# A fp32 transformer stack on one core: three modulation units, two pairs' transposes and products, and a table load are given other places in the attention

## The chip, the cores and the metric

One core of one Trainium2 chip runs the whole program. The time is the device time of one execution in microseconds (us), here the median of three runs. TensorE (PE) does matrix products, VectorE (DVE) and ScalarE (ACT) the elementwise work, GpSimd (POOL) almost nothing, and the queue of SyncE (SP) issues nearly all loads.

## The reference

Two blocks run one after the other on 256 tokens of width 1024, all in fp32. The first has two layers, the second one. Each layer of the first block normalizes, shifts and scales its input with columns of `mod`, mixes tokens (layer 0 by pooling, layer 1 by attention), adds the result through a gate, and does the same around an MLP. The second block is a mix of a gated delta net with a forgetting attention, followed by another MLP. The change lies in layer 1's attention, and by its text in the second block's gates.

```python
mod = c_act @ w_mod[i] + b_mod[i]            # c_act = silu(c), 1 x 1024
sh1, sc1, g1, sh2, sc2, g2 = split(mod, 6)
h = modulate(rmsnorm(x, norm_mix[i]), sh1, sc1)
q, k, v = split(h @ w_qkv, 3)                # 16 heads of 64
logit = q @ k.T / 8 + t5_bias                # causal: one block holds the 256 tokens
o = softmax(logit) @ v
x = x + g1 * (o @ w_o)
h = modulate(rmsnorm(x, norm_mlp[i]), sh2, sc2)
x = x + g2 * (relu(h @ w_up) ** 2 @ w_down)
```

With 256 tokens and blocks of 256, no block lies in the past, so the reference's choice of blocks leaves plain causal attention.

## The kernel before, in words

**Products.** A fp32 product runs as three products of a faster fp32 format: each operand is split into a high part and the rest. For a weight, a piece of 128 x 1024 is loaded as `_r`, ACT copies it into the high part `_h` (line 245), and DVE subtracts to get the low part `_l` (line 251). PE needs both. Pieces that are split within the buffers of the modulation columns carry `_m` or `_p` instead, and have to wait until such a buffer is free.

**Modulation columns.** A unit (`wmc112` to `wmc117` in the attention) is one load of a megabyte, two passes of DVE over it (`column`, line 440) that multiply it with `c_act` and sum along it, and one small fix-up (line 444). None of these columns is needed in the attention; they are for the layer's MLP. Such units are taken one at a time from a list, `pending`, by `ride` (line 944). In the attention the function `riding` (line 1174) calls it, and `riding` itself is called at the end of each of the eight projections of queries and keys and of the two quarters of values, ten calls in all, with six units to hand out: it calls `ride(4)` each time, and the first six calls find one.

**The attention** (`attention`, line 1144). Sixteen heads are worked as eight pairs. PE's program there is: products with `h` for the values and for `qk` (queries and keys, from `wqk`, four projections a half), between them the pairs' scores `s`, transposes `pt` of the softmax's rows, and products `pv` with the values, and last the output products `wo`. `pt5` is head 5's transposes, and `pv2` belongs to heads 4 and 5. Where the small pieces stand among the wide products is set by a clock that counts the estimated cost of the wide steps (`beside`), and a table `events` of (time, piece): a pair's scores are due at `H_S + H_P * head`, its transposes `H_T` after them (`H_TL` for the last four heads), its `pv` `H_V` after the second head's transposes. `until_head` issues all pieces up to a head without regard to the clock. In the attention PE runs in exactly this order (`InOrder`, line 281).

```python
at = H_S + H_P * hd if hd < 12 else max(H_S + H_P * hd, 36.0 + H_S + H_L * (hd - 12))
lag, by = (H_T, H_P) if hd < 12 else (H_TL, H_L)
events += [(at, hd, scores, pr), (at + lag, hd, transposes, hd), (at + lag + by, hd + 1, transposes, hd + 1),
           (at + lag + by + H_V, hd + 1, pv, pr)]
```

**A head's way.** PE writes the scores; DVE adds the bias and takes each row's maximum (`softmax_rows`, line 1110), negates it (line 1112); ACT takes exp with a sum (line 1113); DVE takes reciprocals (line 1114) and scales (line 1115); PE transposes (`pt`); ACT copies the transposed rows to `pT` (line 1210); PE multiplies with the values (`pv`); ACT and DVE split the result into `att_o_hi` and `att_o_lo` (lines 977, 978), which the `wo` products read. Each head has two row blocks, so that sm00 and sm01 are those of head 0, and sm120 the first of head 12.

**The order of the other engines** is set by a scheduler when the program is built; each engine then works its own queue strictly in that order. SP's loads too run in order: a load whose buffer is not free yet holds up those behind it.

**The second block** interleaves the computation of its gates with projections (`interleave`, line 111): after each step of the gates, `R_GATE` steps of the projection. One step of the gates gives the running sums `fc` (line 1444).

Of the kernel before, what the change touches and what calls it, by code (L numbers as in the profile page):

```python
# [8 lines left out]
F32 = mybir.dt.float32  # L9
F32R = mybir.dt.float32r  # L10
I32 = mybir.dt.int32
AF = mybir.ActivationFunctionType
ALU = mybir.AluOpType

P = 128
# [18 lines left out]
B_FIRST = 4 * 128  # L34
B_PREV = 2 * B_FIRST
B_N = B_PREV + 4 * PADW
R_GATE = 2.0
H_S = 1.0
H_P = 2.8
H_L = 2.0  # L40
H_T = 6.5
H_V = 2.0
H_TL = 5.0
DELAY = 3
C_FEAT = 0.6
T2K = 8
R_LEFT = 10
# [60 lines left out]
V_BG, V_POOL = 15, 16  # L108


def interleave(main, filler, ratio=None):

    owed = 0.0
    for r in main:
        owed += r if ratio is None else ratio
        while owed >= 1.0:
            owed -= 1.0
            next(filler, None)
    for _ in filler:
        pass  # L120
# [37 lines left out]
def build(tc, a, out):  # L158
    nc = tc.nc
    vec, act, pe, pool, sp = nc.vector, nc.scalar, nc.tensor, nc.gpsimd, nc.sync  # L160
    from contextlib import ExitStack
    ctx = ExitStack()
    with ctx:
# [4 lines left out]
        work = ctx.enter_context(tc.tile_pool(name="work", bufs=2))  # L168
# [33 lines left out]
        def later():  # L202
            st = ExitStack()
            for f in fences:
                st.enter_context(tc.issue_after(f))
            return st
# [68 lines left out]
        ones = const.tile([P, P], F32, name="ones")  # L275
# [404 lines left out]
        steps = {}  # L680
# [195 lines left out]
        for sec, hf in HALVES:  # L876
            n = f"s{sec}{hf}"
# [66 lines left out]
        def ride(left):  # L944

            if len(pending) > left:
                with later(), tc.issue_after(ride_after[0]) if ride_after else ExitStack():
                    pending.pop(0)()
# [184 lines left out]
        def attention(i, h, w0, wn):  # L1133
# [5 lines left out]
            ohl = hl_tiles("att_o", S)  # L1139
            toep_ap = toep[:, :]  # L1140
            st = {}

            def values(w, t):

                ps = mm_tile(f"v0{t}")
                token_major(w, h, t * P, P, ps)
                act.activation(vt[:, t, :512], ps, AF.Copy)

            def quarter_values(w, q):

                ps = mm_tile(f"v1{q}")
                for t in range(2):
                    for kt in range(KT):
                        mm3(ps[:, t * 256:(t + 1) * 256], hl(h, kt, slice(t * P, (t + 1) * P)),
                            w(q * 2048 + kt * 256, 256), kt == 0, kt == KT - 1)
                        if kt % 2:
                            yield 0.64
                c0 = 512 + q * 256
                act.activation(vt[:, :, c0:c0 + 256], ps.rearrange("p (t d) -> p t d", t=2), AF.Copy)
                riding()  # L1160
# [11 lines left out]
                riding()  # L1172

            def riding():
                ride(4)
                if len(sums_due) > delay[0]:
                    sums_due.pop(0)()

# [51 lines left out]
            def wo(j, t):  # L1230
                if t == 0:
                    wos.append(split_chunk(a["w_o"][j], f"wo{j}", spare=3 * j))
                ts = slice(t * P, (t + 1) * P)
                if j == 0:
                    for n in range(2):
                        wops[t, n] = (mm_tile, acc_tile)[t](f"wo{t}{n}")
                for m in range(8):
                    k, n = (m // 2, m % 2) if j else (m % 4, m // 4)
                    mm3(wops[t, n], hl(ohl, 4 * j + k, ts), wos[j](k * D + n * 512, 512), j == 0 and k == 0,
                        j == 1 and k == 3)  # L1240
                    if m % 2:
                        yield 1.28
# [3 lines left out]
            for pr in range(NH // 2):  # L1246
                hd = 2 * pr
                at = H_S + H_P * hd if hd < 12 else max(H_S + H_P * hd, 36.0 + H_S + H_L * (hd - 12))
                lag, by = (H_T, H_P) if hd < 12 else (H_TL, H_L)
                events += [(at, hd, scores, pr), (at + lag, hd, transposes, hd), (at + lag + by, hd + 1, transposes, hd + 1),  # L1250
                           (at + lag + by + H_V, hd + 1, pv, pr)]
            events.sort(key=lambda e: e[0])

            def beside(steps):

                for cost in steps:
                    clock[0] += cost
                    while events and events[0][0] <= clock[0]:
                        _, _, f, n = events.pop(0)
                        f(n)  # L1260

            def until_head(hd):
                while any(e[1] <= hd for e in events):
                    _, _, f, n = events.pop(0)
                    f(n)
# [6 lines left out]
            pe = InOrder(nc.tensor)  # L1272
            delay[0] = DELAY
            for t in range(2):
                values(w0, t)
            todo = all_projects(0)
            for steps in todo[:2]:
                for _ in steps:
                    pass
            for steps in todo[2:]:  # L1280
                beside(steps)
            todo = all_projects(1)
# [4 lines left out]
            wn.piece(0)  # L1287
            wn.piece(1)
            steps = wo(1, 0)
            for k in range(4):  # L1290
                until_head(9 + 2 * k)
                next(steps)
            next(steps, None)
            while sums_due:
                sums_due.pop(0)()
            pe = nc.tensor
# [23 lines left out]
        h = boundary(ac, lambda: gates[0, 1], *mods(1, 0), hl_tiles("att1", S), 0, "att1")  # L1320
        wu1 = Chunk(a["w_up0"], "wu10", inmraw=2)
        ac, rest = attention(1, h, wv0, wu1)
        while len(pending) > 4:
            ride(4)
# [128 lines left out]
        def conv_proj(chunk, dst, ci):  # L1453
            w = split_chunk(a["w_in"][ci], f"wi{chunk}")
            for h in range(4):
                ps = mm_tile(f"cp{chunk}{h}")[:, :T2]
                yield from costing(ws_steps(w, u, h, ps, 0, T2, 2), 0.68)
                cw = convw[:, ci * 4 + h]
                cb = row272(f"cb{chunk}{h}", T2 + 4)
                y = dst[:, h]  # L1460
                vec.memset(cb[:, 0:3], 0.0)
                act.activation(cb[:, 3:3 + T2], ps, AF.Copy)
                act.activation(y, ps, AF.Copy, scale=cw[:, 3:4])
                for j in range(3):
                    vec.scalar_tensor_tensor(y, cb[:, j:j + T2], cw[:, j:j + 1], y, ALU.mult, ALU.add)
            act.activation(dst, dst, AF.Silu)
            yield 0.0
# [390 lines left out]
        def urgent(gen):  # L1858

            while True:  # L1860
                with tc.high_priority():
                    try:
                        r = next(gen)
                    except StopIteration:
                        return
                yield r

        def early_gates():
            yield from gate_chain()
            for i in range(3):  # L1870
                yield
                gdn_decays(i)

        interleave(urgent(early_gates()), conv_proj(1, gk, 1), R_GATE)

        def rounds(fill, *gens):
# [218 lines left out]
```

## Time and profile before

| | |
|---|---|
| median of 3 runs (946.74, 948.55, 949.04) | 948.55 us |
| the profiled execution | 948.82 us |
| its span, first to last instruction | 947.0 us |
| mean granted clock of PE over the span | 0.990 of full speed |
| PE busy | 913.9 us, 97% of the span |
| DVE busy | 638.7 us, 67% |
| ACT busy | 498.2 us, 53% |
| POOL busy | 12.5 us, 1% |
| moved from and to memory | 198.31 MB, 209 GB/s in the mean |

Of an execution's 948.82 us, 947.0 lie between the first and the last instruction. All times below with a place in the program count from the first instruction. A busy share is that of the whole span. A wait is idle time of an engine, put down to the instruction that ended it. The attention's heads lie between about 275 and 375 us.

### The profile page before, as it was taken

The page shows a single profiled execution, that of the slowest core. Times are in us where ns is not written, and L with a number is a line of the kernel's source. Part 1 is how long each engine was busy: PE and PEld are TensorE (multiplying, and loading weights), DVE is VectorE, ACT ScalarE, POOL GpSimd, SP SyncE. Part 2 cuts the span into 40 slices and gives each one's busy share as a digit, 9 for nine tenths or more (in the row PEclk, how much of TensorE's full clock was granted, in tenths as well). Part 3 has the DMA queues.
Part 4 walks back from the last instruction along what each step waited for, and adds up shares of the span by engine and source line. Part 5 has one row for each costly group of instructions (what it writes and reads, how often), then busy time and mean ns, then how long its engine had stood idle before and what let it go on. Part 6 is the DMA issues. An engine that isn't in the chain of part 4 may idle for free.

```text
span 947.0 us, 15295 instructions
## 1 busy us (share of the span) xinstructions
PE 913.9 (97%) x6045; PEld 795.4 (84%) x6045; DVE 638.7 (67%) x1222; ACT 498.2 (53%) x881; POOL 12.5 (1%) x22
## 2 busy tenths in 40 slices
PE   7999999999998999999999989999999999999996
PEld 3668789989797977889999968899988799999995
DVE  1686899887797765875555667697558764545544
ACT  4476444445555764744455545766555554444442
POOL 0000000000000000000000002000000000000000
PEclk9999999999998999999999999999999999999998
DMA  9998899989194560875565643242112555555541
GB/s 364 420 422 304 311 377 343 351 321 339 58 355 172 164 223 6 324 270 178 178 206 185 237 143 138 91 134 91 46 46 90 199 179 187 192 194 184 178 134 45
DMA packets 34555, 198.31 MB, mean 209 GB/s; under 512 B 4186, under 2 KB 6818, under 8 KB 14002
## 3 DMA queue, kind: packets, MB, share of 16 engines
q1 hardware_dynamic: 34338, 197.27, 58.1%
q8 instruction: 47, 0.77, 0.3%
q14 instruction: 24, 0.20, 0.1%
q10 hardware_dynamic: 146, 0.08, 0.0%
HBM read 196.24 MB, written 1.09 MB: 208 GB/s over the span
## 4 chain that ended last, share of the span: by engine, by line
PE 84%; DVE 6%; DMA 4%; issue 3%; ACT 3%; POOL 0%; SPq 0%; DVEq 0%; POOLq 0%; ACTq 0%
PE up L262 6%; PE up L264 6%; PE up L263 6%; PE dn L264 6%; PE dn L263 6%; PE dn L262 6%; PE gu L263 4%; PE gu L264 4%; PE gu L262 4%; PE qk L291 2%; DMA wms<-in_w_mods_dram 2%; PE fd L262 2%; PE fd L263 2%; PE fd L264 2%; PE cp L262 1%
## 5 line engine op out<-in xcount | busy, mean ns | idle before, releaser
L262 PE MATMUL up<-mlp_hi,wu_h 128*128 128x256 f32 x416 | 118.5, 285 | 0.0
L264 PE MATMUL up<-mlp_hi,wu_l 128*128 128x256 f32 x416 | 117.7, 283 | 0.6 <-DVE wu_l L251 0.6
L263 PE MATMUL up<-mlp_lo,wu_h 128*128 128x256 f32 x416 | 117.9, 284 | 0.0
L245 ACT ACTIVATE wd_h<-wd_r 128x1024 fp32r<-128x1024 f32 x58 | 61.2, 1059 | 66.2 <-PE up L263 42.3
L245 ACT ACTIVATE wu_h<-wu_r 128x1024 fp32r<-128x1024 f32 x58 | 60.8, 1062 | 65.8 <-PE dn L264 47.1
L251 DVE TENSOR_TENSOR wu_l<-wu_r,wu_h 128x1024 fp32r<-128x1024 f32 x58 | 70.3, 1223 | 36.7 <-ACT wu_h L245 36.4
L251 DVE TENSOR_TENSOR wd_l<-wd_r,wd_h 128x1024 fp32r<-128x1024 f32 x58 | 70.8, 1223 | 35.5 <-ACT wd_h L245 35.2
L262 PE MATMUL dn<-wd_h,a 128*128 128x512 f32 x232 | 91.1, 393 | 0.0
L263 PE MATMUL dn<-wd_l,a 128*128 128x512 f32 x232 | 90.8, 392 | 0.0
L262 PE MATMUL gu<-f_hi,wgu_h 128*128 128x256 f32 x320 | 90.7, 283 | 0.0
L264 PE MATMUL gu<-f_hi,wgu_l 128*128 128x256 f32 x320 | 90.6, 283 | 0.0
L263 PE MATMUL gu<-f_lo,wgu_h 128*128 128x256 f32 x320 | 90.6, 283 | 0.0
L264 PE MATMUL dn<-wd_h,a 128*128 128x512 f32 x232 | 90.4, 390 | 0.0
L251 DVE TENSOR_TENSOR wgu_l<-wgu_r,wgu_h 128x1024 fp32r<-128x1024 f32 x44 | 53.6, 1225 | 51.3 <-ACT wgu_h L245 51.3
L262 PEld LDWEIGHTS up<-mlp_hi,wu_h 128*128 128x128 f32 x416 | 79.7, 192 | 1.0 <-issue 0.5
L263 PEld LDWEIGHTS up<-mlp_lo,wu_h 128*128 128x128 f32 x416 | 79.7, 192 | 1.0 <-issue 0.5
L264 PEld LDWEIGHTS up<-mlp_hi,wu_l 128*128 128x128 f32 x416 | 79.7, 192 | 0.8 <-DVE wu_l L251 0.8
L245 ACT ACTIVATE wgu_h<-wgu_r 128x1024 fp32r<-128x1024 f32 x44 | 46.6, 1062 | 61.9 <-PE gu L263 29.4
L262 PEld LDWEIGHTS gu<-f_hi,wgu_h 128*128 128x128 f32 x320 | 61.4, 192 | 0.4
L263 PEld LDWEIGHTS gu<-f_lo,wgu_h 128*128 128x128 f32 x320 | 61.4, 192 | 0.3
L264 PEld LDWEIGHTS gu<-f_hi,wgu_l 128*128 128x128 f32 x320 | 61.4, 192 | 0.0
L264 PEld LDWEIGHTS dn<-wd_h,a 128*128 128x128 f32 x232 | 43.6, 188 | 9.9 <-issue 0.9
(786 smaller groups left out, 2276.6 us busy)
## 6 DMA issues: line engine op xcount, KB each, us to landing
wu_r<-in_w_up_dram SPq DMA_DIRECT2D x32, 1024.0 KB, 6.4
wd_r<-in_w_down_dram SPq DMA_DIRECT2D x32, 1024.0 KB, 6.7
wgu_r<-in_w_gu_dram SPq DMA_DIRECT2D x22, 1024.0 KB, 5.2
wmc<-in_w_modc_dram SPq DMA_DIRECT2D x16, 1024.0 KB, 7.3
wmg<-in_w_modg_dram SPq DMA_DIRECT2D x12, 1024.0 KB, 7.0
wfd_r<-in_w_fd_dram SPq DMA_DIRECT2D x11, 1024.0 KB, 4.8
wi_r<-in_w_in_dram SPq DMA_DIRECT2D x10, 1024.0 KB, 5.3
wms<-in_w_mods_dram SPq DMA_DIRECT2D x16, 512.0 KB, 10.2
```

The costliest lines, as they stand in the source:

```text
L245: act.activation(hi, r, AF.Copy)
L251: vec.tensor_tensor(lo, r, hi.bitcast(F32), ALU.subtract)
L262: pe.matmul(ps, l[0], r[0], start=first, stop=False)
L263: pe.matmul(ps, l[0], r[1], start=False, stop=False)
L264: pe.matmul(ps, l[1], r[0], start=False, stop=last)
L291: f(*a, **k)
```

## The change

Six edits, in words. `riding` counts its calls and hands out a unit only at calls 1, 2, 3, 6, 8 and 10. The first pair's transposes and product are due 1.5 later on the table's clock (`H_FIRST`), and the product of pair 5 is due 1.5 later (`H_VL`). At the end, head 15's transposes and `pv7` are issued ahead of the last six products with the third quarter of the last `wo` chunk instead of behind them. A one-column exponential into a tile that nothing reads (`exp_table`) is written down after the first two projections. The interleaving of the gates takes one ratio for each step.

```diff
--- before.py
+++ after.py
@@ -34,14 +34,17 @@
 B_FIRST = 4 * 128
 B_PREV = 2 * B_FIRST
 B_N = B_PREV + 4 * PADW
-R_GATE = 2.0
+R_GATE = (2.0, 2.0, 4.5, 1.5, 2.0, 3.0)
 H_S = 1.0
 H_P = 2.8
 H_L = 2.0
 H_T = 6.5
 H_V = 2.0
+H_VL = 3.5
+H_FIRST = 1.5
 H_TL = 5.0
 DELAY = 3
+RIDES = (1, 2, 3, 6, 8, 10)
 C_FEAT = 0.6
 T2K = 8
 R_LEFT = 10
@@ -108,11 +111,11 @@
 V_BG, V_POOL = 15, 16
 
 
-def interleave(main, filler, ratio=None):
+def interleave(main, filler, ratios):
 
     owed = 0.0
-    for r in main:
-        owed += r if ratio is None else ratio
+    for n, _ in enumerate(main):
+        owed += ratios[n]
         while owed >= 1.0:
             owed -= 1.0
             next(filler, None)
@@ -1139,6 +1142,7 @@
             ohl = hl_tiles("att_o", S)
             toep_ap = toep[:, :]
             st = {}
+            rode = [0]
 
             def values(w, t):
 
@@ -1172,7 +1176,9 @@
                 riding()
 
             def riding():
-                ride(4)
+                rode[0] += 1
+                if rode[0] in RIDES:
+                    ride(4)
                 if len(sums_due) > delay[0]:
                     sums_due.pop(0)()
 
@@ -1247,8 +1253,9 @@
                 hd = 2 * pr
                 at = H_S + H_P * hd if hd < 12 else max(H_S + H_P * hd, 36.0 + H_S + H_L * (hd - 12))
                 lag, by = (H_T, H_P) if hd < 12 else (H_TL, H_L)
+                lag += H_FIRST if pr == 0 else 0.0
                 events += [(at, hd, scores, pr), (at + lag, hd, transposes, hd), (at + lag + by, hd + 1, transposes, hd + 1),
-                           (at + lag + by + H_V, hd + 1, pv, pr)]
+                           (at + lag + by + (H_V, H_VL)[pr == 5], hd + 1, pv, pr)]
             events.sort(key=lambda e: e[0])
 
             def beside(steps):
@@ -1277,6 +1284,8 @@
             for steps in todo[:2]:
                 for _ in steps:
                     pass
+
+            act.activation(work.tile([P, 1], F32, tag="psum", name="exp_table", bufs=4), ones[:, 0:1], AF.Exp)
             for steps in todo[2:]:
                 beside(steps)
             todo = all_projects(1)
@@ -1287,10 +1296,14 @@
             wn.piece(0)
             wn.piece(1)
             steps = wo(1, 0)
-            for k in range(4):
-                until_head(9 + 2 * k)
-                next(steps)
-            next(steps, None)
+            for hd in (9, 11, 13):
+                until_head(hd)
+                if hd < 13:
+                    next(steps)
+
+            until_head(15)
+            for _ in range(3):
+                next(steps, None)
             while sums_due:
                 sums_due.pop(0)()
             pe = nc.tensor
```

What the built program makes of it shows in the order of each engine. First DVE's queue at the first heads. `wqk01_l0` and `wqk01_l1` are low parts of weights, `wmc115` a modulation unit, sm00 to sm11 the row blocks of heads 0 and 1. The line numbers of the changed kernel are 3 higher. Before the change the rows from that weight's split on are these:

```order
L251 TENSOR_TENSOR wqk01_l0_2804<-wqk01_r0_2801,wqk01_h0_2803 128x1024
L440 ISA wmc115_2795,modcol1_103<-wmc115_2795,crow_96,vecs_84 128x1024
L440 ISA modcol1_103 128x1
L440 ISA wmc115_2795,modcol1_103<-wmc115_2795,crow_96,vecs_84 128x1024
L440 ISA modcol1_103 128x1
L1110 ISA sm0_2597,sm00_m_2598<-s0_2589,toep0_2587 128x128
L1110 ISA sm00_m_2598 128x1
L1110 ISA sm0_2597,sm01_m_2607<-s0_2589,toep0_2587 128x256
L1110 ISA sm01_m_2607 128x1
L1110 ISA sm1_2616,sm10_m_2617<-s1_2592,toep1_2590 128x128
L1110 ISA sm10_m_2617 128x1
L1110 ISA sm1_2616,sm11_m_2626<-s1_2592,toep1_2590 128x256
```

The two passes of `wmc115`, each with the read of its sum, come ahead of the first maximum. With the change DVE's queue reads, from the same split on:

```order
L254 TENSOR_TENSOR wqk01_l0_2801<-wqk01_r0_2798,wqk01_h0_2800 128x1024
L1113 ISA sm0_2599,sm00_m_2600<-s0_2591,toep0_2589 128x128
L1113 ISA sm00_m_2600 128x1
L1113 ISA sm0_2599,sm01_m_2609<-s0_2591,toep0_2589 128x256
L1113 ISA sm01_m_2609 128x1
L1113 ISA sm1_2618,sm10_m_2619<-s1_2594,toep1_2592 128x128
L1113 ISA sm10_m_2619 128x1
L1113 ISA sm1_2618,sm11_m_2628<-s1_2594,toep1_2592 128x256
L1113 ISA sm11_m_2628 128x1
```

The unit `wmc115` no longer stands between the split of a weight and the first heads' maxima; it comes behind `wqk11_l1`. Unit `wmc116`, which stood between the first heads' negated maxima and their reciprocals, now stands among heads 10 and 11.

Next DVE's queue at the last heads. `wo0` and `wu10` are weights, sm12 is head 12. Before the change they stood thus:

```order
L251 TENSOR_TENSOR wo0_l0_3523<-wo0_r0_3520,wo0_h0_3522 128x1024
L251 TENSOR_TENSOR wu10_m0_3639<-wu10_r0_3637,wu10_m0_3639 128x1024
L251 TENSOR_TENSOR wu10_m1_3642<-wu10_r0_3637,wu10_m1_3642 128x1024
L251 TENSOR_TENSOR wo0_l1_3530<-wo0_r0_3520,wo0_h1_3529 128x1024
L978 TENSOR_TENSOR att_o_lo_2385<-pv4_3377,att_o_hi_2384 128x256
L251 TENSOR_TENSOR wo0_l2_3593<-wo0_r2048_3590,wo0_h2_3592 128x1024
L1110 ISA sm12_3426,sm120_m_3427<-s12_3418,toep12_3416 128x128
L1110 ISA sm120_m_3427 128x1
L1110 ISA sm12_3426,sm121_m_3436<-s12_3418,toep12_3416 128x256
L1110 ISA sm121_m_3436 128x1
```

Head 12's maxima come right behind `wo0_l2`. With the change the same stretch of DVE's queue reads:

```order
L254 TENSOR_TENSOR wu10_m0_3641<-wu10_r0_3639,wu10_m0_3641 128x1024
L254 TENSOR_TENSOR wo0_l1_3525<-wo0_r0_3515,wo0_h1_3524 128x1024
L981 TENSOR_TENSOR att_o_lo_2385<-pv4_3374,att_o_hi_2384 128x256
L443 ISA wmc117_3508,modcol1_103<-wmc117_3508,crow_96,vecs_84 128x1024
L443 ISA modcol1_103 128x1
L443 ISA wmc117_3508,modcol1_103<-wmc117_3508,crow_96,vecs_84 128x1024
L443 ISA modcol1_103 128x1
L254 TENSOR_TENSOR wo0_l2_3595<-wo0_r2048_3592,wo0_h2_3594 128x1024
L447 SCALAR_TENSOR_TENSOR modcol1_103<-modcol1_103,vecs_84 128x1
L1113 ISA sm12_3423,sm120_m_3424<-s12_3415,toep12_3413 128x128
L1113 ISA sm120_m_3424 128x1
L1113 ISA sm12_3423,sm121_m_3433<-s12_3415,toep12_3413 128x256
```

Unit `wmc117` now stands behind the low part of `pv4`'s result and ahead of `wo0_l2` and head 12's maxima, and `wu10_m1`, which stood ahead of those, comes after the maxima of heads 12 and 13. Since `wu10_m0` and `wu10_m1` are split in buffers that the units 116 and 117 leave, the two halves of the last `wo` chunk change places in what they wait for: the first now waits for `wo0_l1`, the second for `wu10_m1`.

Last the start of ACT's queue, far ahead of the attention. `n00` and `n01` are sums of squares of the input `x`, `cact` is silu of `c`. Before the change ACT begins so:

```order
L339 ACT_TABLE_LOAD
L339 ACTIVATE n00_sq0_117,n00_ss_116<-x_81 128x512
L339 ACTIVATE n00_sq1_119,n00_ss_116<-x_81 128x512
L339 ACTIVATE n01_sq0_122,n01_ss_121<-x_81 128x512
L417 ACT_TABLE_LOAD
L417 ACTIVATE cact_97<-vecs_84 128x8
```

The first table load belongs to the squares. With the change ACT begins so:

```order
L1288 ACT_TABLE_LOAD
L1288 ACTIVATE exp_table_2568<-ones_89 128x1
L342 ACTIVATE n00_sq0_117,n00_ss_116<-x_81 128x512
L342 ACTIVATE n00_sq1_119,n00_ss_116<-x_81 128x512
L342 ACTIVATE n01_sq0_122,n01_ss_121<-x_81 128x512
L420 ACT_TABLE_LOAD
L420 ACTIVATE cact_97<-vecs_84 128x8
```

The scheduler puts the exponential ahead of everything else on ACT, and the loads of tables that follow stay, the one ahead of the attention's first exponential among them (two places earlier in the queue). Their number is 8 in both programs. In the second block the order of every engine is the same in both.

## Rows read from the trace of the kernel before

**Rows 1.** Waits of PE, whole span: engine, tile, line, what ended it: us, times, longest.

```profile
PE pt L291 <- DVE sm_nm L1112: 3.7, 1, 3.7
...
PE fc L1444 <- DVE logf L1437: 1.4, 1, 1.4
```

**Rows 2.** Busy time by stretch: columns in the first line.

```profile
core 0: us, PE busy (x) PEld busy (x) DVE busy (x) ACT busy (x) POOL busy (x), PEclk, DMA share, GB/s
283.00:293.00 10.00, 6.34 (x33) 5.87 (x32) 8.92 (x39) 4.69 (x16) 0.00 (x0) 0.66 0.83 308
382.00:557.00 175.00, 175.00 (x1094) 157.85 (x1093) 112.97 (x138) 89.86 (x118) 0.53 (x1) 1.00 0.64 222
```

**Rows 3.** Timeline of PE, 283 to 294 us: start, duration, instruction, [wait before it].

```profile
283.26 0.28 PE L291 MATMUL qk<-att_hi,wqk_l 128*128 128x256 f32 x1
287.20 1.13 PE L291 MATMUL pt<-ident,sm 128*128 128x128 f32 x3 [3.66 <-DVE sm_nm L1112]
...
288.35 0.41 PE L291 MATMUL qk<-att_lo,wqk_h 128*128 128x256 f32 x1
...
292.58 0.28 PE L291 MATMUL qk<-att_hi,wqk_h 128*128 128x256 f32 x1
...
293.65 0.49 PE L291 MATMUL pt<-ident,sm 128*128 128x128 f32 x3
```

**Rows 4.** The chain that ended last, 302 to 342 us: start, duration, what.

```profile
302.39 2.15 PE qk L291 x18
...
305.40 0.80 PE pv L291 x8
...
340.19 1.75 ACT sm L1113 x8
```

**Rows 5.** Timeline of DVE, 275 to 334 us.

```profile
275.76 1.28 DVE L440 CUSTOM_DVE_ANT_0 wmc<-wmc,crow,vecs 128x1024 f32<-128x1024 f32 x1
...
278.17 0.29 DVE L1110 CUSTOM_DVE_ANT_0 sm<-s,toep 128x128 f32<-128x128 f32 x1
...
279.28 1.22 DVE L251 TENSOR_TENSOR wqk_l<-wqk_r,wqk_h 128x1024 fp32r<-128x1024 f32 x1
...
280.76 1.28 DVE L440 CUSTOM_DVE_ANT_0 wmc<-wmc,crow,vecs 128x1024 f32<-128x1024 f32 x1
...
286.87 0.28 DVE L1115 TENSOR_SCALAR sm<-sm,sm_rs 128x128 f32<-128x128 f32 x1
...
333.40 0.42 DVE L978 TENSOR_TENSOR att_o_lo<-pv,att_o_hi 128x256 fp32r<-128x256 f32 x1
```

**Rows 6.** Timeline of ACT: the start, the first heads, the last heads.

```profile
4.37 0.63 ACT L339 ACTIVATE n_sq<-x 128x512 f32<-128x512 f32 x1 [1.40 <-DMA x<-in_x_dram]
...
276.66 1.06 ACT L245 ACTIVATE wqk_h<-wqk_r 128x1024 fp32r<-128x1024 f32 x1 [2.53 <-PE qk L291]
...
281.10 1.28 ACT L1113 ACT_TABLE_LOAD   x1
...
338.18 2.01 ACT L245 ACTIVATE wo_p<-wo_r 128x1024 fp32r<-128x1024 f32 x2 [2.44 <-DMA wo_r<-in_w_o_dram]
```

**Rows 7.** Timeline of PE, 331 to 360 us.

```profile
331.40 1.54 PE L291 MATMUL pv<-pT,att_v 128*64 128x256 f32 x8
332.87 0.38 PE L291 MATMUL qk<-att_hi,wqk_h 128*128 128x256 f32 x1
...
340.51 0.65 PE L291 MATMUL pv<-pT,att_v 128*64 128x256 f32 x2
...
343.17 0.39 PE L291 MATMUL v<-wv_h,att_hi 128*128 128x256 f32 x1
...
357.06 1.57 PE L291 MATMUL pv<-pT,att_v 128*64 128x256 f32 x8
...
359.11 0.50 PE L291 MATMUL wo<-wo_h,att_o_hi 128*128 128x512 f32 x1 [0.47 <-ACT att_o_hi L977]
```

**Rows 8.** Loads of tiles `wu_r` and `wo_r`, 235 to 360 us, in that order.

```profile
DMA to landing us min/median/max: 5.0/5.2/5.3
...
DMA to landing us min/median/max: 7.3/7.3/7.3
```

## The prediction

> **What bounds the kernel now.** Read the waits of TensorE (PE) first. PE is busy 97% of the span (the table above), so a change pays only if it removes time in which PE stands still or runs at its lower clock. The longest single wait of PE in the whole execution is the 3.7 us before the transposes `pt` [rows 1]: one wait, in the attention, put down to the softmax on VectorE (DVE).
>
> The table by stretch shows its second half: from 283 to 293 us PE works only 6.3 of 10 us and its granted clock is 0.66, a mean over its two levels, 1.2 and 2.4 GHz [rows 2]. PE's timeline shows why [rows 3]. The last `qk` product before the wait starts at 283.26; `pt` starts at 287.20; the products after it last 0.41 us instead of 0.28 (the lower clock, after the idle time), until at 292.58 they are back at 0.28. From 283.26 to 292.58 are 9.32 us, and between stand `pt`'s three transposes and 22 `qk` products. A run of 18 products at full clock takes 2.15 us, 0.12 each [rows 4], and `pt` 0.49 when nothing is late [rows 3], so the same work takes 22 x 0.12 + 0.49 = 3.1 us. **The place costs 6.2 us**, 3.7 to 3.9 of waiting and the rest clock.
>
> What is late there? DVE's timeline answers [rows 5]. It starts a unit of modulation columns (`wmc115`, two passes) at 275.76, so head 0's score maxima start at 278.17 instead, 2.4 us later; a second unit (`wmc116`) from 280.76 to 283.17 stands between the negated maxima and the reciprocals, a third comes behind. The scaled rows that `pt0` reads are written from 286.87. DVE has no idle time in that stretch; it is a queue in the wrong order, not a slow engine. Nothing after the attention absorbs a gain: from 382 to 557 us PE is busy 175.0 of 175 us [rows 2], so what PE gains moves the end.
>
> **The change, part by part** (times on the clock of the profiled execution).
>
> *Columns ride later, transposes later.* Units 115, 116 and 117 leave the stretch. In the changed order DVE goes from `wqk01_l0` straight to the maxima of heads 0 and 1: 275.76 plus 1.11 (278.17 to 279.28) [rows 5] = 276.9. `wqk01_l1` waits for ScalarE's (ACT's) copy, 276.66 + 1.06 = 277.7 [rows 6], and takes 1.2, to 278.9. ACT's table load of 1.28 us [rows 6], two places earlier in its queue, runs 277.7 to 279.0; four exponentials and the reads of their four sums take 1.75 us [rows 4], so head 0's two take 0.9, to 279.9. Reciprocals and two scalings of some 0.3 each follow: head 0 is ready near 280.9. PE asked for it at 283.4 and now asks 18 products x 0.12 = 2.2 us later, near 285.5. The spare is 4.6 us. I looked for what is late next: head 1 is ready near 282.8 and asked for at 288.7; head 2 is ready near 289.9, behind `wqk11_l1` and the unit 115 (2.4 us) that now follows it, and is asked for at 291.5. The smallest spare is thus 1.6 us, and all 6.2 us should come back.
>
> *The queue of loads.* On SP, unit 117's load is moved behind `toep4` to `toep7` and two weight loads, so these no longer stand behind its wait for unit 115's columns. Behind it now stand `toep8` and the second half of `wv1`; the load is free at about 288.2, and the `wv1` half waits for a DVE product near 292.5 anyway: nothing.
>
> *The units' new places.* Each costs DVE 2.4 us where it lands. Unit 116 lands ahead of the scaling of heads 10 and 11: ready near 330, asked for at 333 and later, nothing. It gives one thing: ACT copies only one quarter of `wu10` before `wo0_h1`, not two, so head 9's copy is 1 us earlier. Unit 117 lands behind `pv4`'s low part (333.40) [rows 5], and pushes back head 12's maxima by 1 us, `wu10_m1`, and with it the load of `wo1`'s second half, whose buffer is now the one that `wu10_m1` frees. Before, ACT waited 2.44 us for `wo1`'s first half with the exponentials queued behind it [rows 6].
>
> *The late part, term by term.* A `pv` takes 0.80 us when nothing is late [rows 4]. Now `pv4` takes 331.40 to 332.87 = 1.47, `pv5` 340.51 to 343.17 = 2.66, and `pv7` with the wait behind it 357.06 to 359.11 = 2.05 [rows 7]: 0.67, 1.86 and 1.25 us lost. `pv4` waited for head 9's copy: +0.67. `pv5` is moved behind the scores of heads 14 and 15, and head 11's copy ahead of the exponentials: +1.86. `pv7` now comes before the six products with `wo1`'s third quarter, which cover the copies of its result; it still waits for head 15's copy: +0.5. New waits: head 12 is now scaled behind head 14's maxima, -0.55 at `pt12`. The load of `wo1`'s second half is issued near 339.0; its landing I bound by the nearest rows, 5.2 us (`w_up`) and 7.3 us (`w_o`) [rows 8], and take 5.2, since it no longer runs beside the first half: 344.2. Behind it on ACT, in its order, come two weight copies, `pv5`'s and head 12's copies, four exponentials and head 13's copy, some 5.0 us: 349.2 against 349.0 at which PE asks, -0.3 with the release. Sum +2.2. Lower end: a landing of 7.3 us takes 2.1 more, +0.1. Upper end: no new wait and the whole of `pv7`, +3.8.
>
> *exp's table loaded ahead.* The scheduler puts the one-column exponential at the very start of ACT's queue, with the silu load after it, so the load ahead of head 0's exponentials remains. At the start its table load takes the place of the first one, and ACT idles 1.40 us there for `x` [rows 6]; one column costs under 0.3 us: nothing. If that cover went, 0.3. Even a load that truly left the attention would take 1.28 us from ACT in front of a head with 4.6 us to spare.
>
> *Gates' running sums.* The new ratios leave the order of every engine in the second block as it was, so the 1.4 us before `fc` [rows 1] stay: nothing.
>
> *Sum.* 6.2 + 2.2 = 8.4 us. The profiled execution took 948.82 us, 0.27 above the median of 948.55; 948.82 - 8.4 = 940.4, against the median 940.2. I forecast **940.2**.
>
> **A rule against the change.** Rows first: the clock was at its lower level after 3.7 us of waiting [rows 3], and stayed up over `pv5`'s 2.66 us, 1.86 of them lost [rows 7]. The new late order puts two scores, `pv5`, a short wait and `pt12` together, 0.86 + 0.80 + 0.55 + 0.49 = 2.7 us without a wide product, then wide ones again. So by the rows the clock should hold, barely; if it fell there, the same price as at `pt0`, 6.2 less 3.7 = 2.5 us, would come off: 942.7.
> The Trainium skill (TensorE: Matmul & The Clock Gate, Part 4: PE-mode transpose) says that transposes don't count as work for the clock in the way that matmuls do; by that rule the cluster comes nearer to idle than its length says, and the sum would be 5.9 instead of 8.4. The rows of the kernel before show no fall behind a cluster this short.
>
> **Rivals.**
> A, forecast: both places pay, 938.5 to 941.9. For: spares of 1.6 us and more, worked out above.
> B, the early place pays, the late one gives nothing: `wo1`'s second half lands after 7.3 us or DVE's new 2.4 us show up at `pt12`. 948.55 - 6.2 = 942.3, with the late term from +0.1 to -0.5 up to 943. For: ACT's 2.44 us behind such a load [rows 6]. Against: fewer loads are in flight.
> C, the clock falls in the late cluster: 942.7.
> D, the wait at `pt0` shrinks to about 1.5 us and PE's clock still falls: 6.2 - 1.5 - 2.5 = 2.2 come back, 944 to 946.3 with the late term between 2.2 and 0. Against: the spare of 4.6 us would have to be wrong by 6.
> E, the change doesn't do what it says, since the table load and the sums aren't moved in the built order and the wait has another cause than the columns: within 0.3% of 948.5 (2.8 us, about what a measurement of this kernel tells from no change). Against: DVE's rows name the columns [rows 5].
> F, slower: the wait moves to `wo1`'s second half. Its load now hangs on `wu10_m1` behind unit 117, and ACT holds head 13's exponentials behind it in order; every us past 344 is a us of PE. It decides only if it lands 8.4 us later, past 352, 13 us after its issue; past 355 the kernel takes 951 or more. Against: the rows of loads of this size, 5.2 to 7.3.
>
> **How the numbers follow.** A 0.58, B 0.15, C 0.06, D 0.08, E 0.08, F 0.05. Faster by over 0.3% are A, B, C and most of D: 0.87; the same is E: 0.08; slower F: 0.05. The range: the low end is all late terms at their best, 948.55 - 6.2 - 3.8 = 938.5, less 0.7, since the fastest of the three runs lies 1.8 below their median: 937.8. The high end takes in B, C and the lower half of D: 945.0. That holds A, B, C and half of D, 0.83.
>
> **What would show it.** Right: no wait of PE before `pt` over 0.5 us; a granted clock near 1.00 from 275 to 290; the products from 293 to 340 us some 6 us earlier; a table load still ahead of the first exponential of the attention; the wait before `fc` unchanged; a wait of under 1 us at `pt12` and at `pv6`; no wait at `pv5`. Wrong: a wait at `pt2` (then unit 115's new place is too early), a wait at `pv6` or `pt14` of 2 us or more with ACT behind `wo1`'s load (B or F), or a lower clock between 340 and 360 (C).

## The result and the profile after

| | before | after |
|---|---|---|
| median | 947.75 us (4 runs, 946.74 to 949.04) | 941.54 us (4 runs, 939.86 to 941.77) |
| profiled execution, its span | 948.82, 947.0 | 941.56, 939.8 |
| mean granted clock | 0.990 | 0.992 |

The ratio is 0.9923, with a 95% interval of 0.9900 to 0.9946: 0.8% faster, about 7.3 us, with the interval from 5.1 to 9.5. The two medians in the table differ by 6.2 us, which lies in it too. Taken again later (experiment e5) the ratio was 0.9921 (0.9898 to 0.9944). Forecast were 8.4 us and 940.2, with a range of 937.8 to 945.0.

The wait that led the list of PE's waits [rows 1] is gone. Of PE's waits for the softmax 0.2 us is left, at head 12, and the wait before `fc` is unchanged:

```profile
PE fc L1457 <- DVE logf L1450: 1.4, 1, 1.4
...
PE pt L294 <- DVE sm L1118: 0.2, 1, 0.2
```

The table by stretch [rows 2], columns as there, shows PE busy without a gap at the first heads and from 340 to 360 us, with its clock up:

```profile
283.00:293.00 10.00, 10.00 (x85) 9.40 (x86) 9.54 (x34) 6.66 (x15) 0.00 (x0) 1.00 0.90 330
...
340.00:360.00 20.00, 20.00 (x97) 15.40 (x96) 9.43 (x25) 8.02 (x22) 0.54 (x1) 1.00 0.29 107
```

Such a table hides lost time where a product is only slow, since a waiting `pv` counts as busy. PE's timeline [rows 3, 7] has the single steps, `pt0`, `pv4`, `pv5`, `pt12`, `pv6` and `pv7` in this order:

```profile
285.73 0.49 PE L294 MATMUL pt<-ident,sm 128*128 128x128 f32 x3
...
325.42 0.87 PE L294 MATMUL pv<-pT,att_v 128*64 128x256 f32 x8
...
336.81 0.87 PE L294 MATMUL pv<-pT,att_v 128*64 128x256 f32 x8
337.85 0.70 PE L294 MATMUL pt<-ident,sm 128*128 128x128 f32 x3 [0.16 <-DVE sm L1118]
...
342.97 1.09 PE L294 MATMUL pv<-pT,att_v 128*64 128x256 f32 x8
...
347.57 1.51 PE L294 MATMUL pv<-pT,att_v 128*64 128x256 f32 x8
349.02 0.74 PE L294 MATMUL wo<-wo_p,att_o_hi 128*128 128x512 f32 x2
```

DVE [rows 5] goes from the weight's split straight to the maxima, and scales head 0 from 280.71 us on:

```profile
274.81 1.21 DVE L254 TENSOR_TENSOR wqk_l<-wqk_r,wqk_h 128x1024 fp32r<-128x1024 f32 x1
275.94 0.28 DVE L1113 CUSTOM_DVE_ANT_0 sm<-s,toep 128x128 f32<-128x128 f32 x1
...
280.71 0.73 DVE L1118 TENSOR_SCALAR sm<-sm,sm_rs 128x128 f32<-128x128 f32 x3
```

ACT [rows 6] has its new table load at the start, in front of the same idle time for `x`, still loads a table ahead of the first exponential of the attention, and waits for the second half of `wo1`:

```profile
1.69 1.28 ACT L1288 ACT_TABLE_LOAD   x1 [1.69 <-PEq L2090]
2.98 0.20 ACT L1288 ACTIVATE exp_table<-ones 128x1 f32<-128x1 f32 x1
4.71 0.63 ACT L342 ACTIVATE n_sq<-x 128x512 f32<-128x512 f32 x1 [1.52 <-DMA x<-in_x_dram]
...
277.93 1.28 ACT L1116 ACT_TABLE_LOAD   x1
...
338.37 1.06 ACT L248 ACTIVATE wo_p<-wo_r 128x1024 fp32r<-128x1024 f32 x1 [1.12 <-DMA wo_r<-in_w_o_dram]
```

**Where the time went.** Two marks that the change does not touch frame the attention: the first heads' scores, and the first product of the MLP behind its last transposes. Before:

```profile
274.19 0.93 PE L291 MATMUL s<-att_k,att_q 64*128 64x128 f32 x8
...
380.75 0.50 PE L262 MATMUL up<-wu_m,mlp_hi 128*128 128x512 f32 x1 [0.79 <-DVE mlp_hi L391]
```

After:

```profile
274.38 0.93 PE L294 MATMUL s<-att_k,att_q 64*128 64x128 f32 x8
...
372.07 0.50 PE L265 MATMUL up<-wu_m,mlp_hi 128*128 128x512 f32 x1 [0.79 <-DVE mlp_hi L394]
```

The attention took 106.56 us and takes 97.69: **8.87 us came back there**, more than forecast. The span is shorter by 7.2 only. Before the attention 0.2 is lost, and 1.5 behind `fc`, at the gates of the second block. There both kernels do the same in the same order, with the same wait of 1.4 us. PE's clock fell behind it in both, but not for as long. Before, by stretches of 2 us (the clock is the third number from the end):

```profile
594.00:596.00 2.00, 2.00 (x17) 0.96 (x15) 2.00 (x4) 1.97 (x5) 0.00 (x0) 1.00 0.04 8
596.00:598.00 2.00, 2.00 (x7) 1.09 (x6) 1.88 (x7) 1.43 (x6) 0.00 (x0) 0.58 0.49 74
598.00:600.00 2.00, 2.00 (x11) 2.00 (x12) 1.45 (x6) 0.56 (x3) 0.00 (x0) 0.57 0.84 319
```

After:

```profile
586.00:588.00 2.00, 2.00 (x11) 1.04 (x9) 2.00 (x4) 1.59 (x3) 0.00 (x0) 0.55 0.04 8
588.00:590.00 2.00, 2.00 (x5) 0.97 (x4) 1.27 (x5) 0.84 (x4) 0.00 (x0) 0.50 0.76 152
590.00:592.00 2.00, 2.00 (x11) 2.00 (x10) 1.00 (x4) 0.83 (x3) 0.00 (x0) 0.50 0.84 341
592.00:594.00 2.00, 2.00 (x14) 2.00 (x13) 0.96 (x6) 0.00 (x0) 0.00 (x0) 0.74 0.11 45
```

What the clock takes from such rows is (1 - granted clock) x 2 us, summed: 2 x (0.42 + 0.43) = 1.7 before, 2 x (0.45 + 0.50 + 0.50 + 0.26) = 3.4 after. Such a sum is lost time only where PE has work in the stretch, as here; where the clock falls while PE still waits, a part of it costs nothing. The experiments ask whether that belongs to the change, and which of its parts gave the 8.87.

### The profile page after: what moved, and what is told of

Its sections match the earlier page's. It is cut to its first block, busy times and chain, and to the rows that moved or that the text cites. A ratio compares the mean times of both kernels' runs of the same rounds, so it can differ in the third digit from the quotient of the medians.

```text
span 939.8 us, 15292 instructions
## 1 busy us (share of the span) xinstructions
PE 911.8 (97%) x6045; PEld 794.0 (84%) x6045; DVE 637.3 (68%) x1222; ACT 497.4 (53%) x882; POOL 12.5 (1%) x22
## 4 chain that ended last, share of the span: by engine, by line
PE 87%; DVE 4%; DMA 3%; issue 2%; ACT 2%; POOL 0%; SPq 0%; DVEq 0%; POOLq 0%; ACTq 0%
PE up L265 6%; PE up L267 6%; PE up L266 6%; PE dn L267 6%; PE dn L265 6%; PE dn L266 6%; PE gu L267 4%; PE gu L266 4%; PE gu L265 4%; PE qk L294 4%; DMA wms<-in_w_mods_dram 2%; PE fd L265 2%; PE fd L266 2%; PE fd L267 2%; PE v L294 1%
```

## The experiments

Length is that of the attention between the two marks. The last three columns are the clock's toll, summed as above over the stretches of one profiled execution: between 30 and 62 us (two places, from 30 to 42 and near 55), at the first heads, at the gates. In every profile the clock also falls at the very end, where PE has nothing left to do; that is not listed. Of the 3.4 at the heads before some 0.8 falls into the wait: the clock is low from about 285.6 us, and PE starts again at 287.20 [rows 3]. Each ratio is against the kernel before on the same chip.

| kernel | median us | ratio (95%) | length | 30-62 | heads | gates |
|---|---|---|---|---|---|---|
| before | | 1 | 106.56 | 1.7 | 3.4 | 1.7 |
| after | 941.54 | 0.9923 (0.9900-0.9946) | 97.69 | 1.7 | 0 | 3.4 |
| e1 units later alone | 941.58 | 0.9919 (0.9897-0.9941) | 97.70 | 5.1 | 0 | 1.7 |
| e2 first transposes later alone | 941.16 | 0.9917 (0.9894-0.9940) | 99.58 | 0 | 0 | 0 |
| e3 late part alone | 947.00 | 0.9980 (0.9962-0.9998) | 103.10 | 1.7 | 1.7 | 0 |
| e4 table load and ratios alone | 946.55 | 0.9976 (0.9963-0.9989) | 104.52 | 3.4 | 1.7 | 1.7 |
| e5 after, again | 940.69 | 0.9921 (0.9898-0.9944) | 97.58 | 3.4 | 0 | 1.7 |
| e6 units, `pv7` | 940.47 | 0.9923 (0.9897-0.9949) | 97.17 | 3.4 | 0 | 1.7 |
| e7 after, sums behind | 941.52 | 0.9929 (0.9905-0.9952) | 97.88 | 1.7 | 0 | 1.7 |
| e8 after, gates spread | 939.78 | 0.9904 (0.9879-0.9930) | 97.41 | 3.4 | 0 | 0 |
| e9 e6, sums behind, silu | 939.80 | 0.9919 (0.9894-0.9944) | 97.17 | 0 | 0 | 0 |
| e10 e6, gates spread, silu | 937.11 | 0.9892 (0.9871-0.9914) | 97.20 | 1.7 | 0 | 0 |
| e11 unit 115 left early | 940.82 | 0.9925 (0.9895-0.9954) | 99.36 | 0 | 0 | 1.7 |
| e12 unit 115 at call 5 | 940.06 | 0.9921 (0.9897-0.9945) | 97.76 | 5.1 | 0 | 1.7 |

### The parts one by one

**e1**, the kernel before with the list of calls and nothing else:

```diff
+RIDES = (1, 2, 3, 6, 8, 10)
...
+            rode = [0]
...
             def riding():
-                ride(4)
+                rode[0] += 1
+                if rode[0] in RIDES:
+                    ride(4)
```

> The kernel before with only the six units handed out at calls 1, 2, 3, 6, 8 and 10. Mark: the start of the last eight transposes of the MLP's input, at 378.87 us before and 370.19 after. Theory (the units on VectorE are what was late): no wait of PE before the first heads' transposes, full clock from 283 to 293 us, all 6.2 us of the early place come back without the later transposes; behind pv4 another 0.7. With pv5, pv7 unmoved and unit 117 ahead of head 12's maxima, the late part gives 0 to 0.7. Mark near 372.4, time about 941.5 to 942.5. Rival (units and later transposes are needed together): a wait of about 1 us and a lower clock stay, mark 375 to 377.

Measured: 97.70, the length of the whole change. Theory held for the early place: there is no wait before `pt0`, the granted clock is 1.00 at the heads, and heads 4 and 5's scores come 15.67 us behind the first (22.03 before).

```profile
286.00 0.49 PE L292 MATMUL pt<-ident,sm 128*128 128x128 f32 x3
```

It missed the late place: `pv5`, unmoved, takes 0.90 us up to the next product, and so loses almost nothing.

```profile
336.10 0.97 PE L292 MATMUL pv<-pT,att_v 128*64 128x256 f32 x8
337.00 0.39 PE L292 MATMUL v<-wv_h,att_hi 128*128 128x256 f32 x1
...
339.31 0.93 PE L292 MATMUL s<-att_k,att_q 64*128 64x128 f32 x8
```

With the units away, head 11's copy stands ahead of the four exponentials in ACT's queue, and that is what `pv5` had waited for:

```profile
335.69 0.47 ACT L1214 ACTIVATE pT<-pt 128x384 f32<-128x384 f32 x1
...
337.00 0.39 ACT L1114 ACTIVATE sm<-sm,sm_nm 128x128 f32<-128x128 f32 x1
```

**e2**, only the first pair later:

```diff
+                lag += 1.5 if pr == 0 else 0.0
```

> The kernel before with only the first pair's transposes and product due 1.5 later on the clock. Theory: head 0's rows are still ready only at 287.2 us, PE asks 18 products (2.2 us) later, so a wait of 1.5 us stays before the transposes. If the clock still falls behind it, 2.2 us come back (mark 376.7); if 1.5 us are too short for a fall, 4.7 (mark 374.2). Rival: the wait alone is the whole cost and the clock is never lowered by so short a wait; or the later heads turn late and nothing comes back (mark 378 to 379).

Measured: no wait at all before `pt0`, length 99.58, 6.98 us back.

```profile
284.30 0.49 PE L291 MATMUL pt<-ident,sm 128*128 128x128 f32 x3
```

Heads 4 and 5's scores come 15.69 us behind the first: this edit alone gives the whole early place, as e1 does. By its time (0.9917) it can't be told from e1 or from the changed kernel, though its length is 1.9 over e1's. Neither theory had that, and the reason is not on PE. With a later date for `pt0` the scheduler also writes DVE's queue in another order:

```profile
274.53 1.28 DVE L440 CUSTOM_DVE_ANT_0 wmc<-wmc,crow,vecs 128x1024 f32<-128x1024 f32 x1
...
276.94 0.28 DVE L1110 CUSTOM_DVE_ANT_0 sm<-s,toep 128x128 f32<-128x128 f32 x1
...
283.04 0.28 DVE L1115 TENSOR_SCALAR sm<-sm,sm_rs 128x128 f32<-128x128 f32 x1
...
285.60 1.27 DVE L440 CUSTOM_DVE_ANT_0 wmc<-wmc,crow,vecs 128x1024 f32<-128x1024 f32 x1
```

Unit 115 is still ahead of the maxima, but unit 116 now comes behind head 0's scaling, which starts at 283.04 and not at 286.87 [rows 5]. The expectation took DVE's order as fixed; it is not, even where the edit names PE alone.

**e3**, the late part alone: pair 5's product 1.5 later, head 15's transposes and `pv7` ahead of six products, as in the diff of the change.

> The kernel before with only pair 5's product 1.5 later on the clock and head 15's transposes with pv7 ahead of the last six products of the third quarter. Theory: pv5 loses nothing (1.86 us back), pv7 half of its loss (0.6 back), head 12 is not late since unit 117 stands elsewhere: mark 376.4, time 2.5 us below before. Rival (the late part pays only with the units moved, since weights' copies on ScalarE and the load of the last chunk are what is late): mark 378 to 379, no change.

Measured: length 103.10, 3.46 less. Of that some 1.2 is not of the late part. Up to the `qk` product behind `pv4`, at 332.87 before and 332.15 here, all is in the same order, but the clock at the first heads was lowered for less long (toll 1.7, not the 3.4 of which 0.8 fell into the wait). That gives 1.0, and a shorter `pv4` the other 0.2. 2.2 remain, somewhat less than theory's 2.5. The ratio, 0.9980, shows 1.9 us. So this part pays where the units are as before, and `pv5` there loses nothing:

```profile
342.76 0.87 PE L291 MATMUL pv<-pT,att_v 128*64 128x256 f32 x8
```

**e4**, the exponential and the list of ratios alone, as in the diff.

> The kernel before with only the one-column exponential and the list of ratios. Theory: nothing, mark 378.9, time within 0.5 us of before; the wait before the running sums stays at 1.4 us. What it tells beside: how far the runs of one order of work scatter, and in how many of them TensorE's clock is lower for longer behind the running sums (7 us in the profile after, 3.5 in that of before). Rival: the table load ahead of the input's squares or the ratios move something, 1 us or more to either side, and the long stretch of lower clock in the profile after comes from them.

Measured: length 104.52; of the 2.04 us 0.9 again came by a shorter fall of the clock at the first heads, 0.4 from a shorter `pv4`, and 0.8 from `pv5`, whose wait for head 11's copy was 0.43 us, not 1.2. The ratio, 0.9976, says some 2 us faster, which the theory of nothing doesn't hold and the order of work doesn't explain: the queues of the second block are those of before. Twelve runs lie between 945.42 and 948.72, those of before on this chip between 945.40 and 952.41. What made the long times rarer here stays open.

### The clock's toll, and the gates

**e5**, the changed kernel once more.

> The changed kernel itself, again, beside its variants. Length of the attention, from the first heads' scores to the first product of the MLP behind its last transposes: 106.56 us before, 97.69 after, 97.70 with the units alone. Theory: 97.7 again, and what differs between executions is how much TensorE's lower clock costs at three places (near 55 us, the first heads, the gates near 590 us), 0, 1.7 or 3.4 us at each in the profiles so far; time 941 within 1.5. Rival: the 3.4 us lost behind the running sums in the first profile of this kernel belong to its order of work, and come again.

Measured: 1.7 at the gates, not 3.4; the rival falls. In fourteen profiled executions the toll at any one of these places is 0, 1.7 or 3.4 us, and the gates of one order of work gave 1.7 (before, e1, e4, e5, e6, e11, e12), 3.4 (after) and 0 (e2, e3).

**e6**, units and `pv7`, without the two later dates (`H_FIRST`, `H_VL`), table load and ratios: the change's last hunk on e1.

> The units later and head 15's transposes with pv7 ahead of the last six products of the third quarter; pv5 and the first pair's transposes where they were. Theory: moving pv5 gives nothing once the units are moved (with them alone it lost 0.1 us) and costs 0.35 at head 12 and 0.2 at pv6, while pv7's move gives 0.6: length of the attention 97.1, half a us under the changed kernel. Rival: the parts only pay together, length 97.7 or more.

Measured: 97.17, as worked out. By its time it can't be told from the changed kernel.

**e7 and e8**, on the changed kernel. Its ratios had left the order as it was, so `fc` is fenced to stand behind the projection products written so far (e7 with 8.0 as third ratio, e8 with 10.0, which also spreads the gate products):

```diff
-R_GATE = (2.0, 2.0, 4.5, 1.5, 2.0, 3.0)
+R_GATE = (2.0, 2.0, 8.0, 1.5, 2.0, 3.0)
...
+            behind = last_on(mybir.EngineType.PE)
...
-                    pe.matmul(fc[:FH, c0:c0 + c], logf[:cj, j], rhs, start=j == 0, stop=j == i)
+                    with tc.issue_after(behind):
+                        pe.matmul(fc[:FH, c0:c0 + c], logf[:cj, j], rhs, start=j == 0, stop=j == i)
```

> The changed kernel with the running sums and the gate products behind them issued behind the next 24 projection products (2.9 us of work), by an order on TensorE, since the ratios alone left the order as it was. Theory: the wait of 1.4 us before the sums goes, and with it the lower clock behind them; 1.4 and 0 to 3.4 us (1.7 in the middle) come back: time 937.5 to 939.5. Rival 1: the many small products lower the clock by themselves, 1.4 at most. Rival 2: the gates' results are now late for the next step, and nothing or less than nothing is left.

> As the one before, with more projection steps written ahead, so that the gate products behind the running sums stand among wide products instead of in one cluster. Theory: same gain, 937.5 to 939.5, since the wait is what lowers the clock. Rival 1 (the small products lower it): here it stays up, there not, and this one is 1.7 us or more faster than the other. Rival 2: the gates come later still and the next step waits for them.

Measured: the wait before `fc` is gone in both, and a new one is there, 1.9 us in e7 and 1.5 in e8. In e7 PE waits for ACT:

```profile
600.06 0.45 PE L265 MATMUL cp<-u_hi,wi_h 128*128 128x272 f32 x1 [1.90 <-ACT gv L1478]
```

And ACT's timeline shows why. The keys' silu slipped between the gates' exponentials, so two more tables are loaded (10 instead of 8), and the copies of PE's results come behind them:

```profile
594.46 1.28 ACT L1481 ACT_TABLE_LOAD   x1
595.75 1.11 ACT L1481 ACTIVATE gqk<-gqk 128x1088 f32<-128x1088 f32 x1
596.87 1.28 ACT L1533 ACT_TABLE_LOAD   x1
...
599.51 0.50 ACT L1478 ACTIVATE gv<-cp,convw 128x272 f32<-128x272 f32 x1
```

The clock stayed up over the cluster of small gate products (1.00 from 582 to 598 us in e7) and fell only behind the new wait:

```profile
582.00:598.00 16.00, 16.00 (x118) 13.72 (x117) 10.39 (x30) 11.93 (x22) 0.00 (x0) 1.00 0.22 69
598.00:600.00 2.00, 0.16 (x2) 0.00 (x0) 0.79 (x2) 1.99 (x7) 0.00 (x0) 1.00 0.00 0
600.00:602.00 2.00, 1.94 (x9) 1.94 (x10) 1.93 (x4) 1.62 (x4) 0.00 (x0) 0.56 0.35 61
```

Both missed their time: 941.52 and 939.78 us, where 937.5 to 939.5 was expected. In e7 nothing of the gain is left, as rival 2 had it, though ACT's copies are late and not the gates' results. e8 is 1.7 us faster than e7, the mark of rival 1, but the rows of e7 don't bear rival 1 out: the clock fell behind the wait, not over the cluster. In e8 it stayed at 1.00 behind its wait of 1.5 us.

**e9 and e10** are e6 with e7's or e8's sums, the last three ratios 0, and the silu fenced behind the last exponential of the gates:

```diff
+            gates_end.append(last_on(mybir.EngineType.Activation))
...
-            act.activation(dst, dst, AF.Silu)
+            with tc.issue_after(gates_end[0]) if chunk == 1 else ExitStack():
+                act.activation(dst, dst, AF.Silu)
```

> Units later, head 15's transposes and pv7 ahead of the last six products, the running sums and gate products behind the next 24 projection products, and the silu of the keys behind the gates' exponentials, so that ScalarE loads 8 tables again and not 10. Theory: what took the sums' gain away in the two kernels before was the wait of 1.5 to 1.9 us for ScalarE's copies behind two more table loads; without them no wait of over 0.5 us is left near 580 to 605 us, the clock stays up there, and from the MLP's first product to g2kk it takes 239.7 us (241.0 in the profiles with the sums' wait and no fall, 242.6 with one). Length of the attention 97.2. Time 937 to 939.5. Rival: the cluster of small gate products lowers the clock without a wait: 1.7 us more, 939 to 941.

> As the one before, with the gate products spread among wide products. Theory: the same, 239.7 and 937 to 939.5, since no wait stands there in either. Rival 1 (the cluster lowers the clock): this one is 1.7 us faster. Rival 2: the keys' silu stands ahead of the copies of the next projection's results here, and the wait for ScalarE comes back in part: 0.5 to 1.5 us slower than the other.

Measured, the wait of PE that is left there, in e9 and then in e10:

```profile
PE cp L263 <- ACT gv L1474: 0.6, 1, 0.6
```

```profile
PE cp L263 <- ACT gv L1474: 0.2, 1, 0.2
```

From the MLP's first product to `g2kk` e9 takes 240.5 and e10 240.2 us (239.7 expected), against 242.6 in e5, and the two profiled spans are both 935.5. The clock did not fall at the gates in either. Yet e9's runs reach from 937.27 to 943.19, e10's from 936.18 to 939.43. That fits the rival, a cluster that lowers the clock in some executions; but falls between 30 and 62 us, which took 5.1 us in e1 and e12, would do as well. Only one execution of e9 is profiled, so the place of its falls is not shown. e9's time (939.80) lies above what was expected and in its rival's range, and by the ratio it (0.9919) can't be told from e6 (0.9923). e10 (937.11, as expected; 0.9892) is the fastest of all. Its slowest run lies below the fastest of the changed kernel (939.86), but that ran on another chip, and the intervals of their ratios overlap (0.9871 to 0.9914 against 0.9900 to 0.9946): **that e10 beats the changed kernel is likely, not shown.**

### Which unit it was

**e11** is e1 with the calls (1, 2, 3, 4, 8, 10), **e12** with (1, 2, 3, 5, 8, 10).

> The kernel before with the units at calls 1, 2, 3, 4, 8 and 10: unit 115 stays ahead of the first heads' maxima, the two after it leave the stretch. In the built order the scaling of head 0 stands behind the maxima of heads 2 and 3, whose scores PE writes until 282.6 us of the first profile. Theory: one unit of 2.4 us alone costs little: head 0 is ready 0.5 to 1 us after PE asks, the clock stays up after so short a wait, and the early place (first scores to second pair of units' third scores) gives back 5.2 to 5.7 of 6.2; length of the attention 98.2 to 98.9. Rival: any wait there lowers the clock, 1.7 or 3.4 us more.

> The units at calls 1, 2, 3, 5, 8 and 10: one unit stands between the first heads' negated maxima and their scaling, as unit 116 did before, and none ahead of the maxima. Theory: ready within 0.3 us of when PE asks, 5.9 to 6.2 of 6.2 back, length of the attention 97.7 to 98.1: it takes both units to make the wait of 3.7 us. Rival: the place behind the maxima is the one that counts, a wait of over 1 us stays and the clock falls.

Measured in e11:

```profile
283.41 0.88 PE L292 MATMUL pt<-ident,sm 128*128 128x128 f32 x3 [1.08 <-DVE sm_nm L1113]
```

```profile
280.00:290.00 10.00, 8.80 (x72) 7.94 (x71) 7.04 (x32) 8.05 (x22) 0.00 (x0) 1.00 0.96 366
```

One unit ahead of the maxima leaves a wait of 1.08 us, a little over the 0.5 to 1 expected, and a length of 99.36 (98.2 to 98.9 expected), 1.66 over e1's. The clock stays up behind it, so this wait costs itself, the 0.4 by which `pt0` is slower, and some 0.2 in which the product ahead of it runs out with none beside it. In e12 there is no wait and the length is 97.76, 0.06 over e1's. It takes both units in the stretch to make the 3.7 us.

## Why the prediction was right, and where its sizes were off

**The early place** was forecast at 6.2 us. Heads 4 and 5's scores came 22.03 us behind the first scores before (296.22 - 274.19) and come 15.69 behind after (290.07 - 274.38): 6.3. The steps held. The maxima run from 275.94 to 277.05 (275.8 to 276.9 forecast), the table load runs from 277.93 to 279.21 (277.7 to 279.0), head 0 is scaled by about 281.2 (280.9), PE asks at 285.73 (285.5). That the units are the cause, e1 shows alone, and e11 and e12 that it takes two of them.

**The late part** was forecast at 2.2 and gave 2.5 to 2.7: `pv4` 0.67 as forecast; `pv5` 1.86 as forecast; `pt12` loses 0.16 in waiting and 0.21 in a slower transpose (0.55 forecast); `pv6` 0.2 (0.3 forecast); `pv7` keeps 0.65 of its 1.25 (349.02 - 347.57 - 0.80), so 0.6 came back (0.5 forecast). The load of `wo1`'s second half was issued at 333.1, some 1 us later than forecast (339.0 less the 6.8 gained ahead of it), and landed in 5.3 us (5.2 taken); rival F had no case. But the reason given for `pv5` named two edits, and e1 shows that the units alone do it: with them moved, the move of `pv5` is worth nothing. The change's length is that of its list of calls; `H_FIRST` and `H_VL` are spare. Without them e6 has 97.17 us, against 97.41 to 97.88 in the four profiles with both.

**The rule on transposes.** The cluster of `s14`, `pv5` and `pt12` now stands from 335.96 to 338.30 us, ahead of the stretch from 340 to 360 that the prediction named. The granted clock over both is 1.00:

```profile
330.00:376.00 46.00, 44.55 (x238) 34.98 (x238) 30.24 (x88) 27.52 (x63) 1.08 (x2) 1.00 0.37 127
```

So rival C is out, and the rule that was weighed against the change (the Trainium skill, TensorE: Matmul & The Clock Gate, Part 4: PE-mode transpose), by which the sum would have been 5.9 us, finds no price in this trace. With three short transposes in the cluster (0.70 us) it is a weak test of that rule.

**The step that was mis-sized is "Gates' running sums: nothing".** For the order it is right: the wait is 1.4 us in both. But the step carried over the clock of one execution as if it belonged to the order. Behind that wait the toll was 1.7 us in the profile before and 3.4 in the one after, and in e5, the same program, 1.7. The longer fall made the profile after 1.5 us longer behind `fc`; with the 0.2 ahead of the attention, that is what lies between 8.87 us there and 7.2 in the two spans. The same holds for the price of the early place: 3.4 us of toll at the heads in the first profile, 1.7 in e3 and e4, where the place thus cost 5.3 and 5.5 by the scores' distance (20.99 and 21.14 less 15.69), not 6.3. The median of many executions would hold both kinds. This would account for a ratio that gives 7.3 us, and for 941.5 where 940.2 was forecast; with three profiles of the order before at the heads, and an interval that holds 8.4 too, it is not shown. That the two spans agree with the ratio is in part luck: the one execution had the longer fall at the heads, the other at the gates.

**The table load** at the start hid as said: ACT idles 1.52 us for `x` behind it (1.40 before), and the load ahead of the attention's exponentials stayed.

## What to carry to other kernels

Where a long wait of PE is put down to a vector engine that has no idle time in front of it, look at what stands in its queue ahead of the late instruction; moving work that nobody waits for behind it, by one list of calls, gave all that six edits gave. Test the parts alone, since two edits can each cure the same wait (e1 and e2 the early one, e1 and e3 that of `pv5`), and read the built order after each, since a later date on one engine reorders another. A wait in front of slow small products costs more than its length in some executions: price it from several profiles, not from one.

## What the runs showed of the hardware

In one and the same order of work TensorE's clock fell behind a wait in some executions and not in others, and the toll came in steps of 1.7 us: 0, 1.7 or 3.4 at each of the places listed, in fourteen profiles. The runs of the kernel before spread over some 7 us on one chip (945.27 to 952.04). The clock fell behind waits of 3.7 and 1.9 us, behind the 1.4 at the gates in eight of ten profiles that have it, and near 55 us, where the products are small and a wait is 1.1, in eleven of fourteen. It did not fall behind the wait of 1.08 among wide products in e11, nor behind the 1.5 in e8, where the gates' small products are spread among wide ones. A table load on ACT took 1.28 us, and in e7 two more of them stood ahead of the copies for which PE waited 1.9 us.
